# Interleaving the Strassen products of neighbouring feed-forward units in the pairs whose C11 came first

## The chip, the cores and the metric

The kernel runs on one core of a Trainium2 chip. The metric is the time of one execution on the device in microseconds (us). The version before the change takes 1913.47 us, the median of three runs (1908.57 to 1915.0). TensorE (PE in the profile) does the matrix products and writes them to PSUM, VectorE (DVE) and ScalarE (ACT) move and combine data, GpSimd (POOL) and SyncE (SP) issue transfers here.

## The reference

One decoder layer over 1024 tokens of width 1024, in float32: a SwiGLU feed-forward block added at half weight, a mixing block (dilated windowed attention beside a latent attention), and a second SwiGLU block.

```
h = rms(x, g)
x = x + 0.5 * (silu(h @ w_gate) * (h @ w_up)) @ w_down      # D_MODEL 1024, D_FF 2816
x = x + W_out [rms(dilated(h)) ; rms(mla(h))]
x = x + 0.5 * swiglu_2(rms(x))
```

The change touches only the gate and up products of the two feed-forward blocks, which the same function `ffn` computes twice.

## The kernel before

**Split products.** Each float32 product is made of three TensorE products in a faster number format: `split` (lines 99 to 102) makes a high part on ScalarE (L101) and the rest on VectorE (L102, called the low part below), and `products` (lines 117 to 127) multiplies high by high, high by low and low by high (L122, L124, L126). A 128x512 result with four blocks of depth is so 12 matmuls into one PSUM bank; `product` does this for one weight operand.

**Seven products instead of eight.** Gate and up weights are taken in 11 pairs (c = 0 to 10) of 128-column blocks; a pair has two units, gate "g" and up "u". For each unit the two column blocks, the two halves of the depth and the two halves of the tokens form a 2x2 by 2x2 block product, and Winograd's form of Strassen's scheme needs seven products for it: M11, M12, S1, S3, S2, S4, M22. The names are those of the weight operands. S1 to S4 are sums of weight blocks that VectorE makes (L328): S1 = M21 + M22, S3 = M11 - M21, S2 = S1 - M11, S4 = M12 - S2. The other factors (B11, B21, B22, T1 to T4) are kept for all 11 pairs.

**Two kinds of pairs.** For the first four pairs (c < FRONT = 4) the M11 and M12 products are done ahead, in `front`, since they need only the first half of the tokens; the product M11 is stored to DRAM (p1) for later. The middle stage then does five products for each unit of these pairs, 60 matmuls. Pairs 4 to 10 do all seven in the middle stage, 84 matmuls for a unit.

**A unit in the middle stage.** `middle` takes two PSUM banks, Dk and E, does S1 into Dk, S3 into E and S2 into a third bank A. Then VectorE reads: a = stored M11 (a tile `kept`, fetched by a POOL transfer, L579) + A (L586), q = a + E (L587), q = q + Dk (L588). `close` goes on in the same banks: S4 is added on top of Dk, and M22 on top of E, so these two products may begin only when L588 and L587 have read the banks. VectorE adds a to each (L596, L600). ScalarE applies the SiLU to the gate's four results (L604), and `finish` multiplies gate and up (L373), forms sums for the later down product (L385 to L388) and stores them with POOL transfers (L377, L383, L389, L390).

**Order.** `order` is a list of all weight operands in the order in which the products use them. `prepare` makes operands up to six products ahead of their use; making S1 of a unit also asks for the raw weights of the next unit (two transfers of 512 KB on SP's queue, L286). `behind_operands` puts the reads of PSUM on VectorE behind the low part of the operand three products on. The matmuls are issued in program order; the other engines' instructions are ordered by the compiler's scheduler. Buffers come from pools: 47 SBUF slots of 4 KB a partition, 12 smaller temporaries (`tmp`), 8 PSUM banks.

**The order in pairs 0 to 3 before.** For each unit in turn: S1, S3, S2, S4, M22. The last unit of a pair, u, is closed by `close_up` at the head of the next pair, directly behind its S2. Pairs 4 to 10 have 24 matmuls of another unit's M11 and M12 between S2 and S4 of a unit.

Of the kernel before, what the change touches and what calls it, by code (L numbers as in the profile page):

```python
# [18 lines left out]
P = 128  # L19
# [4 lines left out]
NF = DFF // P  # L24
# [25 lines left out]
FRONT = 4  # L50
# [11 lines left out]
def tile_layer(ctx: ExitStack, tc: tile.TileContext, x, g1n, mixn, g2n, wg1, wu1, wd1, wg2, wu2, wd2,  # L62
# [27 lines left out]
    def tmp(shape, dt=F32):  # L90
        return tpool.tile(shape, dt, tag="tmp", name=nm("tmp"))
# [131 lines left out]
    def ffn(rows_in, ys, gain, wg, wu, wd, act_d, xsrc, done, lead, aside=iter(())):  # L223
# [66 lines left out]
        PAIRS = range(NF // 2)  # L290
        order = [(c + i, m, w) for c in range(0, FRONT, 2) for w in ("M11", "M12") for i in range(2) for m in "gu"]
        for c in PAIRS:
            if c >= FRONT:
                order += [(c, "g", w) for w in ("M11", "M12")]
            if c > 0:
                order += [(c - 1, "u", w) for w in ("S4", "M22")]
            order += [(c, "g", w) for w in ("S1", "S3", "S2")]
            if c >= FRONT:
                order += [(c, "u", w) for w in ("M11", "M12")]
            order += [(c, "g", w) for w in ("S4", "M22")]  # L300
            order += [(c, "u", w) for w in ("S1", "S3", "S2")]
        order += [(NF // 2 - 1, "u", w) for w in ("S4", "M22")]
        units = [(True, c, m) for c in range(FRONT) for m in "gu"] + [(False, c, m) for c in PAIRS for m in "gu"]
        raws, sums_, ready = {}, {}, {}
# [8 lines left out]
        def make(c, nme, which):  # L313
            front = c < FRONT and which in ("M11", "M12")
            u = (front, c, nme)
            load_units(units.index(u) + (3 if front else 2))
            f1, f2 = raws[u][0], raws[u][-1]
            m = {"M11": f1[:, :512], "M12": f1[:, 512:], "M21": f2[:, :512], "M22": f2[:, 512:]}
            need = {"S1": ("M21", "M22", ALU.add), "S2": ("S1", "M11", ALU.subtract),
                    "S3": ("M11", "M21", ALU.subtract), "S4": ("M12", "S2", ALU.subtract)}  # L320
            if which in need:

                a_, b_, op = need[which]
                if which == "S1":
                    sums_["S1"] = tmp([P, 512])
                s1 = sums_["S1"]
                src = {"S1": s1, "S3": m["M21"], "S2": s1, "S4": m["M12"]}[which]
                nc.vector.tensor_tensor(src, s1 if a_ == "S1" else m[a_], s1 if b_ == "S2" else m[b_], op=op)  # L328
            else:
                src = m[which]  # L330
            s = slot([P, 2, 512], F32R)
            lows.append(split(s[:, 0, :], s[:, 1, :], src))
            ready[(c, nme, which)] = (s[:, 0, :], s[:, 1, :])
            if which == "M22" or (front and which == "M12"):
                del raws[u]
# [13 lines left out]
        def product(pt, c, nme, which, blk, first=True, ahead=AHEAD):  # L349
            assert order[used[0]] == (c, nme, which)  # L350
            prepare(ahead + 1)
            used[0] += 1
            w = ready.pop((c, nme, which))
            products(pt, [(cut(w, k * P, (k + 1) * P), blk.hi_lo(k)) for k in range(4)], first,
                     tc.keep_in_program_order)
# [3 lines left out]
        def finish(f, th, gate, up):  # L359

            c, j = f // 2, f % 2
            if c not in acts:
                acts[c] = {}
            two = acts[c]
            key = "diagonal" if j == th else "other"
            if c < FRONT and j == th == 0:
                early = tmp([P, 512])
                nc.vector.tensor_tensor(early, gate, up, op=ALU.mult)
                nc.gpsimd.dma_start(act_d[0, c], early)
                return  # L370
            if key not in two:
                two[key] = [slot([P, 2, 512]), 0]
            nc.vector.tensor_tensor(two[key][0][:, th if j == th else j, :], gate, up, op=ALU.mult)  # L373
            two[key][1] += 1
            if key == "diagonal" and c < FRONT:
                nc.gpsimd.dma_start(two[key][0][:, 0, :], act_d[0, c])
                nc.gpsimd.dma_start(act_d[3, c], two[key][0][:, 1, :])  # L377
                two[key][1] = 2
            elif key == "diagonal" and two[key][1] == 2:
                nc.gpsimd.dma_start(act_d[0:4:3, c].rearrange("s p t -> p s t"), two[key][0])  # L380
            if len(two) == 2 and two["diagonal"][1] + two["other"][1] == 4:
                (a11, a22), (a21, a12) = ([two[x][0][:, i, :] for i in range(2)] for x in ("diagonal", "other"))
                nc.gpsimd.dma_start(act_d[1, c], a12)  # L383
                s12, s43 = slot([P, 2, 512]), slot([P, 2, 512])
                nc.vector.tensor_tensor(s12[:, 0, :], a21, a22, op=ALU.add)  # L385
                nc.vector.tensor_tensor(s12[:, 1, :], s12[:, 0, :], a11, op=ALU.subtract)
                nc.vector.tensor_tensor(s43[:, 1, :], a11, a21, op=ALU.subtract)
                nc.vector.tensor_tensor(s43[:, 0, :], a12, s12[:, 1, :], op=ALU.subtract)  # L388
                nc.gpsimd.dma_start(act_d[4:6, c].rearrange("s p t -> p s t"), s12)  # L389
                nc.gpsimd.dma_start(act_d[2:7:4, c].rearrange("s p t -> p s t"), s43)  # L390
                del acts[c]
# [169 lines left out]
        def start(c, nme):  # L561

            A, Bk = ps(), ps()
            product(A, c, nme, "M11", B11)
            product(Bk, c, nme, "M12", B21)
            q = tmp([P, 512])
            nc.scalar.activation(q, A, AF.Copy)
            with behind_operands():
                nc.vector.tensor_tensor(q, q, Bk, op=ALU.add)  # L569
            return A, q  # L570

        def middle(c, nme, A):

            Dk, E = ps(), ps()
            product(Dk, c, nme, "S1", T1)
            product(E, c, nme, "S3", T3)
            if c < FRONT:
                A, kept = ps(), tmp([P, 512])
                nc.gpsimd.dma_start(kept, p1_d[c, :, "gu".index(nme), :])  # L579
            product(A, c, nme, "S2", T2, first=c < FRONT)  # L580
            a, q = tmp([P, 512]), tmp([P, 512])
            if c >= FRONT:
                nc.scalar.activation(a, A, AF.Copy)  # L583
            with behind_operands():
                if c < FRONT:
                    nc.vector.tensor_tensor(a, kept, A, op=ALU.add)  # L586
                nc.vector.tensor_tensor(q, a, E, op=ALU.add)  # L587
                nc.vector.tensor_tensor(q, q, Dk, op=ALU.add)  # L588
            return Dk, E, a, q

        def close(c, nme, Dk, E, a, between):

            product(Dk, c, nme, "S4", B22, first=False)
            q = tmp([P, 512])
            with behind_operands():
                nc.vector.tensor_tensor(q, a, Dk, op=ALU.add)  # L596
            between(q)
            product(E, c, nme, "M22", T4, first=False)
            with behind_operands():
                nc.vector.tensor_tensor(a, a, E, op=ALU.add)  # L600
            return q, a

        def silu(q):
            nc.scalar.activation(q, q, AF.Silu)  # L604

        def close_up(c, Dk, E, a, g12, g21):
            _, q = close(c, "u", Dk, E, a, lambda q: finish(2 * c, 1, g12, q))
            finish(2 * c + 1, 0, g21, q)

        late = None  # L610
        for c in PAIRS:
            if c in (4, 6):
                next(aside, None)
            A = Au = None
            if c >= FRONT:
                A, g11 = start(c, "g")
                silu(g11)
            if late:
                close_up(*late)
            Dk, E, a, g22 = middle(c, "g", A)  # L620
            silu(g22)
            if c >= FRONT:
                Au, u11 = start(c, "u")
                finish(2 * c, 0, g11, u11)
            if c == NF // 2 - 1:
                B11.t = B21.t = None
                for _ in range(2):
                    load_down(*loads.pop(0))
            g12, g21 = close(c, "g", Dk, E, a, silu)
            silu(g21)  # L630
            if c == KD - 1:
                fetch(2)
                for _ in range(PRELOAD - 2):
                    load_down(*loads.pop(0))
            Du, Eu, au, u22 = middle(c, "u", Au)
            finish(2 * c + 1, 1, g22, u22)
            late = (c, Du, Eu, au, g12, g21)
# [800 lines left out]
```

## Time and profile before

| what | before |
|---|---|
| median of three runs | 1913.47 us |
| the profiled execution, its own time | 1916.01 us |
| its span, first to last instruction | 1914.2 us |
| TensorE busy | 1835.1 us (96%) |
| VectorE busy | 1245.8 us (65%) |
| ScalarE busy | 793.8 us (41%) |
| mean granted TensorE clock | 0.983 |

The middle stage of pairs 0 to 3 is at about 62 to 206 us of the span in the first feed-forward block and at about 1287 to 1428 us in the second. In a timeline row the first number is the start and the second the duration in us, then engine, line, operation, tiles and count; the bracket says how long the engine had stood idle and whose end released it. In a row of windows stand the stretch, its length, the busy time of the engine with its instructions in brackets, and PEclk, the granted TensorE clock as a share of full speed. A row of waits ends with total us, count and the longest.

### The profile page before, as it was taken

Reading aid. Unit: us, or ns where it says so; the run is one execution under the profiler, and the core shown is the slowest. Engines: PE = TensorE matmul, PEld = TensorE weight load, DVE = VectorE, ACT = ScalarE, POOL = GpSimd, SP = SyncE. Lnnn points to the kernel's source line nnn. Section 1 sums busy time; section 2 is a strip of 40 time slices with the busy share of each in tenths; the row PEclk is TensorE's granted clock in tenths of the full one; section 3 lists DMA queues with packets and bytes.
Section 4 is the critical chain, followed back from the end, with each engine's and each line's share of the span. In section 5 each row is a group of like instructions: output and inputs, shape, how many; then the busy total and the mean of one; then the engine's idle time right before and its main releaser. Section 6 shows DMA issues by size and latency. Waiting matters only on the chain.

```text
span 1914.2 us, 25117 instructions
## 1 busy us (share of the span) xinstructions
PE 1835.1 (96%) x9040; PEld 1548.7 (81%) x9040; DVE 1245.8 (65%) x2375; ACT 793.8 (41%) x1802; POOL 294.8 (15%) x508
## 2 busy tenths in 40 slices
PE   8888999999999999999998999997889999999998
PEld 6666888888888888889998988886678888888887
DVE  6857666665978273327888783467657665778671
ACT  7412323333445153235875672453223333334540
POOL 3011010000000022323354520211000000000000
PEclk9889999999999999999999999998999999999999
DMA  7334224324954241023311332333432332288422
GB/s 253 116 105 156 92 90 138 131 84 176 356 172 127 94 137 33 28 55 117 89 36 30 93 118 77 125 130 117 131 109 96 119 105 94 84 305 310 126 56 88
DMA packets 92326, 234.38 MB, mean 122 GB/s; under 512 B 12487, under 2 KB 18329, under 8 KB 92201
## 3 DMA queue, kind: packets, MB, share of 16 engines
q1 hardware_dynamic: 71592, 162.93, 26.3%
q0 software_dynamic: 20608, 69.85, 10.4%
q8 instruction: 71, 1.16, 0.2%
q14 instruction: 55, 0.44, 0.1%
HBM read 165.00 MB, written 63.53 MB: 119 GB/s over the span
## 4 chain that ended last, share of the span: by engine, by line
PE 85%; DVE 9%; ACT 2%; issue 2%; DMA 2%; POOL 1%; SPq 0%; DVEq 0%; ACTq 0%; POOLq 0%
PE ps L122 18%; PE ps L124 18%; PE ps L126 18%; PE ps L520 7%; PE ps L519 7%; PE ps L518 7%; DVE slot L102 2%; PE ps L847 2%; PE ps L873 1%; PE ps L821 1%; PE ps L912 1%; ACT slot L101 1%; PE ps L837 1%; PE ps L1035 1%; DMA slot<-in_wu_dram 1%
## 5 line engine op out<-in xcount | busy, mean ns | idle before, releaser
L122 PE MATMUL ps<-slot,slot 128*128 128x512 f32 (+3 forms) x1712 | 668.4, 391 | 48.7 <-DVE tmp L588 31.8
L124 PE MATMUL ps<-slot,slot 128*128 128x512 f32 (+3 forms) x1712 | 662.1, 387 | 3.6 <-DVE slot L102 3.6
L126 PE MATMUL ps<-slot,slot 128*128 128x512 f32 (+3 forms) x1712 | 661.5, 387 | 0.0
L122 PEld LDWEIGHTS ps<-slot,slot 128*128 128x128 f32 x1712 | 327.1, 191 | 118.5 <-issue 36.5
L124 PEld LDWEIGHTS ps<-slot,slot 128*128 128x128 f32 x1712 | 327.8, 191 | 66.6 <-DVE slot L102 4.4
L126 PEld LDWEIGHTS ps<-slot,slot 128*128 128x128 f32 x1712 | 326.7, 191 | 63.9
L102 DVE TENSOR_TENSOR slot<-slot,slot 128x512 fp32r<-128x512 f32 (+1 forms) x428 | 294.4, 704 | 36.1 <-ACT slot L101 33.9
L101 ACT ACTIVATE slot<-slot 128x512 fp32r<-128x512 f32 (+1 forms) x428 | 260.7, 638 | 104.3 <-PE ps L520 44.8
L101 ACT ACTIVATE slot<-tmp 128x512 fp32r<-128x512 f32 x258 | 160.5, 626 | 314.1 <-DVE tmp L328 211.0
L519 PE MATMUL ps<-slot,slot 128*128 128x512 f32 x616 | 239.8, 390 | 0.0
L520 PE MATMUL ps<-slot,slot 128*128 128x512 f32 x616 | 239.5, 389 | 0.0
L518 PE MATMUL ps<-slot,slot 128*128 128x512 f32 x616 | 237.1, 389 | 0.0
L102 DVE TENSOR_TENSOR slot<-tmp,slot 128x512 fp32r<-128x512 f32 x258 | 176.4, 687 | 21.6 <-ACT slot L101 21.3
L520 PEld LDWEIGHTS ps<-slot,slot 128*128 128x128 f32 x616 | 115.7, 188 | 24.1
L519 PEld LDWEIGHTS ps<-slot,slot 128*128 128x128 f32 x616 | 115.7, 188 | 23.9
L518 PEld LDWEIGHTS ps<-slot,slot 128*128 128x128 f32 x616 | 115.7, 188 | 23.8
L604 ACT ACTIVATE tmp<-tmp 128x512 f32<-128x512 f32 x80 | 50.6, 632 | 185.9 <-DVE tmp L596 87.5
L526 DVE SCALAR_TENSOR_TENSOR slot<-ps,slot 128x512 f32<-128x512 f32 x56 | 37.4, 688 | 81.4 <-PE ps L520 81.2
L596 DVE TENSOR_TENSOR tmp<-tmp,ps 128x512 f32<-128x512 f32 x44 | 30.3, 688 | 80.3 <-PE ps L126 79.8
L587 DVE TENSOR_TENSOR tmp<-tmp,ps 128x512 f32<-128x512 f32 x44 | 30.2, 686 | 65.4 <-ACT tmp L583 65.2
L569 DVE TENSOR_TENSOR tmp<-tmp,ps 128x512 f32<-128x512 f32 x28 | 19.3, 688 | 81.4 <-PE ps L126 81.4
L829 ACT ACTIVATE slot<-slot,tmp 128x256 f32<-128x256 f32 (+1 forms) x128 | 59.7, 468 | 27.2 <-DVE tmp L822 26.4
(180 smaller groups left out, 2033.6 us busy)
## 6 DMA issues: line engine op xcount, KB each, us to landing
tmp<-act SPq DMA_DIRECT2D x154, 256.0 KB
act<-slot POOLq DMA_DIRECT2D x58, 512.0 KB, 5.2
slot<-in_wg_dram SPq DMA_DIRECT2D x52, 512.0 KB
slot<-in_wu_dram SPq DMA_DIRECT2D x52, 512.0 KB
slot<-in_wd_dram SPq DMA_DIRECT2D x40, 512.0 KB
slot<-in_x_dram SPq DMA_DIRECT2D x16, 512.0 KB
x_mid<-slot POOLq DMA_DIRECT2D x16, 512.0 KB, 4.1
slot<-x_mid SPq DMA_DIRECT2D x16, 512.0 KB
```

Source lines behind the costliest of these rows:

```text
L101: nc.scalar.activation(hi, src, AF.Copy)
L102: return nc.vector.tensor_tensor(lo, src, hi.bitcast(F32), op=ALU.subtract)
L122: pin(nc.tensor.matmul(pt, ah, bh, start=first and i == 0, stop=False, skip_group_check=not first))
L124: pin(nc.tensor.matmul(pt, ah, bl, start=False, stop=False, skip_group_check=not first))
L126: pin(nc.tensor.matmul(pt, al, bh, start=False, stop=i == total - 1, skip_group_check=not first))
L518: nc.tensor.matmul(banks[i], ah, w[:, 0, :], start=first and k == 0, stop=False, skip_group_check=not first)
L519: nc.tensor.matmul(banks[i], ah, w[:, 1, :], start=False, stop=False, skip_group_check=not first)
L520: nc.tensor.matmul(banks[i], al, w[:, 0, :], start=False, stop=k == KD - 1, skip_group_check=not first)
L526: nc.vector.scalar_tensor_tensor(xv, pt, 0.5, xv, op0=ALU.mult, op1=ALU.add)
L604: nc.scalar.activation(q, q, AF.Silu)
L829: nc.scalar.activation(self.p[:, e, :w], self.p[:, e, :w], AF.Exp, bias=self.m[e], scale=-1.0, accum_out=self.den[e])
L847: nc.tensor.matmul(po[:, e * HD:(e + 1) * HD], self.pt[:, n * P:(n + 1) * P], self.head["values"](self.far, self.j, e, j - nb + 1), start= ...
```

## The change

In pairs 0 to 3 the products are put in another order. Each unit does S1 and S3; then come S4 and M22 of the unit before it; then its own S2. `middle` gets a function `between` that is called between S3 and S2: in the gate's turn it closes the preceding pair's up unit (`close_up`), in the up's turn the same pair's gate unit (`close_gate`). The first unit has none before it, and the last, u of pair 3, is closed in pair 4 as before. The sum S1 is kept for each unit (`sums_[u]`), since two are now alive at once. The number of products, sums, reads and transfers is unchanged, and pairs 4 to 10 keep their order.

```
@@ order
+            if c < FRONT:
+                for m in "gu":
+                    order += [(c, m, w) for w in ("S1", "S3")]
+                    if (c, m) != (0, "g"):
+                        order += [(c, "g", w) if m == "u" else (c - 1, "u", w) for w in ("S4", "M22")]
+                    order.append((c, m, "S2"))
+                continue
+            order += [(c, "g", w) for w in ("M11", "M12")]
+            order += [(c - 1, "u", w) for w in ("S4", "M22")]
             order += [(c, "g", w) for w in ("S1", "S3", "S2")]
...
@@ make
                 if which == "S1":
-                    sums_["S1"] = tmp([P, 512])
-                s1 = sums_["S1"]
+                    sums_[u] = tmp([P, 512])
+                s1 = sums_[u]
...
-        def middle(c, nme, A):
+        def middle(c, nme, A, between=lambda: None):
             Dk, E = ps(), ps()
             product(Dk, c, nme, "S1", T1)
             product(E, c, nme, "S3", T3)
+            between()
             if c < FRONT:
                 A, kept = ps(), tmp([P, 512])
                 nc.gpsimd.dma_start(kept, p1_d[c, :, "gu".index(nme), :])
...
-        late = None
-        for c in PAIRS:
...
+        late, part = None, {}
+        def close_gate():
+            part["g12"], part["g21"] = close(*part.pop("g"), silu)
+            silu(part["g21"])
+        for c in range(FRONT):
...
+            Dk, E, a, g22 = middle(c, "g", None, lambda: late and close_up(*late))
+            silu(g22)
+            part["g"] = (c, "g", Dk, E, a)
+            Du, Eu, au, u22 = middle(c, "u", None, close_gate)
+            finish(2 * c + 1, 1, g22, u22)
+            late = (c, Du, Eu, au, part["g12"], part["g21"])
+        for c in range(FRONT, NF // 2):
...
+            A, g11 = start(c, "g")
+            silu(g11)
+            close_up(*late)
             Dk, E, a, g22 = middle(c, "g", A)
             silu(g22)
...
```

More of the change, by code (lines that the diff above doesn't have):

```diff
@@ L292, in ffn @@
         for c in PAIRS:
[L293 to L296, printed above, removed]
+            if c < FRONT:
[7 more added lines that the diff above has]
+            order += [(c - 1, "u", w) for w in ("S4", "M22")]
             order += [(c, "g", w) for w in ("S1", "S3", "S2")]
-            if c >= FRONT:
-                order += [(c, "u", w) for w in ("M11", "M12")]
+            order += [(c, "u", w) for w in ("M11", "M12")]
             order += [(c, "g", w) for w in ("S4", "M22")]
@@ L608, in close_up @@
             finish(2 * c + 1, 0, g21, q)
-        late = None
-        for c in PAIRS:
+        late, part = None, {}
[3 more added lines that the diff above has]
+        for c in range(FRONT):
             if c in (4, 6):
                 next(aside, None)
[L614 to L619, printed above, removed]
+            Dk, E, a, g22 = middle(c, "g", None, lambda: late and close_up(*late))
[5 more added lines that the diff above has]
+        for c in range(FRONT, NF // 2):
+            if c in (4, 6):
+                next(aside, None)
+            A, g11 = start(c, "g")
+            silu(g11)
+            close_up(*late)
             Dk, E, a, g22 = middle(c, "g", A)
             silu(g22)
-            if c >= FRONT:
-                Au, u11 = start(c, "u")
-                finish(2 * c, 0, g11, u11)
+            Au, u11 = start(c, "u")
+            finish(2 * c, 0, g11, u11)
             if c == NF // 2 - 1:
```

## The prediction

> **What bounds the kernel now.** I read the page's head first, then what TensorE waits for over the whole span, then the clock.
>
> ```profile
> span 1914.2 us, 25117 instructions
> PE 1835.1 (96%) x9040; PEld 1548.7 (81%) x9040; DVE 1245.8 (65%) x2375; ACT 793.8 (41%) x1802; POOL 294.8 (15%) x508
> PEclk9889999999999999999999999998999999999999
> ```
>
> ```profile
> PE ps L122 <- DVE tmp L588: 31.8, 12, 3.3
> PE ps L122 <- ACT slot L101: 13.7, 2, 7.5
> ```
>
> TensorE is busy 96% of the span, so it sets the end, and what can be won by another order is where it stands still or runs below its clock. Its largest wait for one line is for L588, the last VectorE read of the bank Dk: 31.8 us in 12 places. The clock row has its low digits in the second and third slice (48 to 144 us) and in one near 1390 us, that is, in both middle stages. One such place, TensorE and VectorE together:
>
> ```profile
> 151.52 0.39 PE L126 MATMUL ps<-slot,slot 128*128 128x512 f32 x1
> 151.95 0.69 DVE L586 TENSOR_TENSOR tmp<-tmp,ps 128x512 f32<-128x512 f32 x1 [0.34 <-PE ps L126]
> 152.55 0.69 DVE L102 TENSOR_TENSOR slot<-slot,slot 128x512 fp32r<-128x512 f32 x1
> 153.15 0.68 DVE L587 TENSOR_TENSOR tmp<-tmp,ps 128x512 f32<-128x512 f32 x1
> 153.87 0.69 DVE L588 TENSOR_TENSOR tmp<-tmp,ps 128x512 f32<-128x512 f32 x1
> 154.70 0.77 PE L122 MATMUL ps<-slot,slot 128*128 128x512 f32 x1 [2.79 <-DVE tmp L588]
> 157.76 0.40 PE L124 MATMUL ps<-slot,slot 128*128 128x512 f32 x1
> ```
>
> S2 ends at 151.91; L586, L587 and L588 follow one another on VectorE, and only then may S4 add to Dk, 2.79 us later. After that, matmuls start 0.43 us apart until 157.76, where they were 0.23 us apart before: the clock had gone down in the wait.
>
> To weigh both together I cut the stage into stretches of one unit, from the start of one S4 to that of the next, 60 matmuls each. The first row is an undisturbed stretch of 60 matmuls; two sums close the seven stretches of each block, 80.21 to 205.94 and 1306.95 to 1427.67.
>
> ```profile
> 200.01:213.61 13.60, 13.60 (x62) 1.00 0.11 40
> ...
> 80.21:99.12 18.91, 16.59 (x60) 0.85 0.18 56
> 99.12:117.36 18.24, 15.45 (x61) 0.89 0.56 182
> ...
> 189.51:205.94 16.43, 16.43 (x61) 0.83 0.22 68
> sum 125.73, PE 109.85; mean PE 15.69
> ...
> 1306.95:1325.22 18.27, 15.96 (x60) 0.87 0.19 58
> ...
> 1343.40:1359.55 16.15, 13.84 (x60) 1.00 0.22 72
> ...
> 1411.25:1427.67 16.42, 16.42 (x60) 0.82 0.20 74
> sum 120.72, PE 104.85; mean PE 14.98
> ```
>
> 14 stretches take 125.73 + 120.72 = 246.45 us, where 14 x 13.60 = 190.4 us would do: 56.05 us are lost. 31.8 of them are the 12 waits, the other 24.25 us are matmuls at a lower clock (a last stretch, 16.43 us, has no wait in it and loses 2.83 us by the clock alone).
>
> **The change, term by term.** Number of matmuls, VectorE operations and transfers: unchanged, cost 0.
>
> *Term 1, the 12 waits for L588: 31.8 us off.* Behind S2 now come S1 and S3 of the next unit, 24 matmuls or 24 x 13.60 / 60 = 5.44 us, in banks of their own. The longest wait so far was 3.3 us. The cover is 2.1 us longer than that, so S4 should find Dk read. If the cover failed, each place would cost its 2.3 to 3.3 us again. E is read by L587, earlier still.
>
> *Term 2, the low clock behind these waits.* The slow matmuls of the first stretch of each block belong to another wait (term 3). In it:
>
> ```profile
> 99.12 0.47 PE L122 MATMUL ps<-slot,slot 128*128 128x512 f32 x1 [2.32 <-DVE tmp L588]
> ```
>
> ```profile
> 1325.22 0.77 PE L122 MATMUL ps<-slot,slot 128*128 128x512 f32 x1 [2.31 <-DVE tmp L588]
> ```
>
> 18.91 - 13.60 - 2.32 = 2.99 us and 18.27 - 13.60 - 2.31 = 2.36 us, together 5.35 us. So 24.25 - 5.35 = 18.9 us stand behind the 12 waits, and go with them. Bounds: 0, if the low clock had another cause, and 18.9. I take 18.9, since slow matmuls begin at the end of waits only, and undisturbed stretches show 1.00.
>
> The Trainium skill, page "TensorE: Matmul & The Clock Gate", section "Why this matters for your kernels", says otherwise about short waits: TensorE falls to half clock when it idles for more than about 3 us. By that, only the two waits of over 3.3 us explain their slow stretches (2.83 and 2.82 us), and the rest, 13.2 us, would stay. The trace does not agree: 2.32 us idle before 99.12 is followed by a stretch at 0.89, though 2.31 us before the stretch at 1343.40 is followed by one at 1.00.
>
> *Term 3, the first unit.* Here VectorE is behind with operands, and S4 of g0 stands far longer:
>
> ```profile
> 72.30 0.39 PE L126 MATMUL ps<-slot,slot 128*128 128x512 f32 x1
> 80.21 0.76 PE L122 MATMUL ps<-slot,slot 128*128 128x512 f32 x1 [7.53 <-ACT slot L101]
> ```
>
> ```profile
> 75.77 0.69 DVE L102 TENSOR_TENSOR slot<-tmp,slot 128x512 fp32r<-128x512 f32 x1
> ...
> 79.38 0.69 DVE L588 TENSOR_TENSOR tmp<-tmp,ps 128x512 f32<-128x512 f32 x1
> ```
>
> ```profile
> 1300.20 0.63 PE L126 MATMUL ps<-slot,slot 128*128 128x512 f32 x1
> 1306.95 0.77 PE L122 MATMUL ps<-slot,slot 128*128 128x512 f32 x1 [6.12 <-ACT slot L101]
> ```
>
> ```profile
> 1302.52 0.69 DVE L102 TENSOR_TENSOR slot<-tmp,slot 128x512 fp32r<-128x512 f32 x1
> ```
>
> The release is put down to ScalarE, but L588 ends at 80.07, 0.14 us before: the same wait, later. In the new order TensorE goes on with S1 of u0. Its low part is the row at 75.77; with the low parts of S4 and M22 of g0 no longer ahead of it (2 x 0.60 us, the spacing of the rows above), it is there at 75.77 + 0.69 - 1.2 = 75.3 us. 24 matmuls at the same slow start end at 75.3 + 5.44 + 2.99 = 83.7 us, after L588; before, 24 matmuls were done at 80.21 + 5.44 + 2.99 = 88.6. Gain 4.9 us. In the second block: 1302.0 + 7.80 against 1306.95 + 7.80, gain 4.9 us. Bounds for both: 0 (VectorE keeps the old order of operands and S1 comes no sooner than S4 did) and 13.7 + 5.35 = 19 us (no wait at all). I take 9.8.
>
> *Term 4, new waits.* VectorE must now do a pair in less time. Two units before:
>
> ```profile
> 136.32:172.18 35.86, 30.74 (x120) 24.59 (x120) 22.24 (x36) 7.97 (x13) 4.18 (x7) 0.90 0.38 125
> ```
>
> ```profile
> DVE tmp L596 <- PE ps L126: 8.0, 2, 4.6
> ```
>
> The third busy time is VectorE's: 22.24 us for a pair that TensorE will do in 2 x 13.60 = 27.2 us, 82%, and in the 35.86 us it waited 8.0 for S4 alone. It fits, but it works in order, and a read that waits for S4 or M22 (L596, L600) holds the operands behind it. Bounds: 0 and all 12 old waits back. I put in two of the fourteen places at 2.3 us, 4.6 us.
>
> Sum: 31.8 + 18.9 + 9.8 - 4.6 = 55.9 us. The profiled execution took 1916.0 us, so 1860.1; the median of the runs lies 2.5 us under it, so **1858 us**.
>
> **Rivals.**
>
> *VectorE becomes the bound in these pairs.* If it keeps only the 8.0 us of waits for S4, a pair takes 22.24 + 8.0 = 30.2 us, 3.0 more than TensorE, for 7 pairs (3.5 in each block) 21 us: 1879. For it speaks the order of its queue; against it, that the 12 waits for L588 all lie in the stretches above, and pairs 4 to 10, with the same reads and 24 matmuls in between, have none.
>
> *The stored M11 comes late.* `kept` (L579) now stands behind `between` in the program, so behind the stores of `finish` on POOL's queue, which wait for VectorE.
>
> ```profile
> 145.26 0.68 DVE L600 TENSOR_TENSOR tmp<-tmp,ps 128x512 f32<-128x512 f32 x1
> ```
>
> ```profile
> 137.84 0.54 POOL L579 DMA_DIRECT2D tmp<-p  x1
> ...
> 149.86 0.71 POOL L390 DMA_DIRECT2D act<-slot  x1 [0.53 <-DVE slot L388]
> 150.56 0.57 POOL L579 DMA_DIRECT2D tmp<-p  x1
> ```
>
> ```profile
> tmp<-p POOLq DMA_DIRECT2D x16, 256.0 KB, 4.1
> ```
>
> From L600 to L579 behind the stores are 5.3 us, and 4.1 to land: 9.4 us after M22's read. L586 wants it 2.7 us after (S2's length), so 6.7 late; cover less chain is 5.44 - 3.3 = 2.1, a wait of 4.6 us, with 18.9 / 12 = 1.6 us of low clock, in the three gate units behind a `close_up` in each block: 6 x 6.2 = 37 us, 1895. Against it: the row at 137.84 was issued ahead of the stores at 149.86, though they stood before it in the program already; nothing it needs has changed.
>
> *The low clock stays.* If slow matmuls behind the ten shorter waits have another cause, 18.9 less those of the last two stretches, 2.83 and 2.82 us, that is 13.2 us, are not won: 1871. For it speaks the stretch at 1343.40, full clock after a wait; against it, that no slow stretch begins without one. The Trainium skill's rule above would have it so.
>
> *It does not do what it says:* VectorE's scheduler puts other work in front of L586 until the 5.44 us are used up; then nothing is won but the first unit, at most: 1904 to 1913, about no change.
>
> *Slower: raw weights starve.* M22 of a unit is now nine operands behind its S1, not five, so its two raw slots are held longer, and the transfers for a coming unit wait for slots.
>
> ```profile
> DMA packets 92326, 234.38 MB, mean 122 GB/s; under 512 B 12487, under 2 KB 18329, under 8 KB 92201
> ```
>
> ```profile
> 126.00 3.05 SPq L286 DMA_DIRECT2D slot<-in_wg_dram  x2
> ```
>
> ```profile
> 159.72 0.68 DVE L328 TENSOR_TENSOR tmp<-slot 128x512 f32<-128x512 f32 x1
> ```
>
> If slots allowed only two units, weights would be asked for when M22 of the last but one is split: 3.05 us to issue, 1 MB at the page's mean 122 GB/s 8.6 us, sum and split three operations of 0.7 us: 13.7 us, against M22 and S2, 5.4 us, as cover. 8.3 + 1.6 us of low clock in 14 units is 139 us, less the 60.5 of terms 1 to 3: 1992. It decides when a unit waits over 60.5 / 14 = 4.3 us. Against it: weights asked for at 126.00 are first summed at 159.72, 33.7 us on. Four operands more cost 4 x 2.72 = 10.9 us of such a lead; at the new pace two units are 27.2 us, and 16 remain.
>
> **How the numbers follow.** Forecast 0.67 (its own range 1846 to 1872, term 4 between 0 and 14 and term 3 up to 15); VectorE as the bound 0.12; late M11 0.08; clock stays 0.04; no change 0.05; slower 0.04. A measurement of this kernel can tell about 0.3% from no change, 5.7 us. Faster is the first four, 0.91; the same 0.05; slower 0.04. The range takes in the forecast, the VectorE case and the clock case and leaves out late M11, no change and slower, 0.17: 1846 to 1886.
>
> **What would show it.** Right: the wait of L122 for L588 gone or down to one or two places; stretches of 60 matmuls at 13.6 to 14 us and PEclk at 1.00 from about 90 to 206 us; VectorE 80% busy there; the first block's down stage some 28 us earlier, the end 56. Wrong in term 1: L122 still waits for L588, or for L102 or L101 instead. Wrong in term 2: no waits, but PEclk under 0.95. Late M11: L586 waits for a transfer, and L579 stands behind L390. Starving: L328 waits for a transfer from the weights.

## The result

The changed kernel takes 1850.99 us, the median of four executions (1850.05 to 1852.3), beside 1911.49 us for the kernel before on the same chip (1908.57 to 1915.0). The ratio is 0.9683, with a 95% interval of 0.9663 to 0.9704: 60.5 us faster, where 1858 us were forecast from 1913.47, 55.5 us. Two executions far outside the others, one of the kernel before at 2076.64 us and one of the kernel with useless matmuls (below) at 3766.56 us, are left out of all that follows.

The page of the changed kernel, its first lines and its clock row:

```profile
span 1848.6 us, 25118 instructions
PE 1812.8 (98%) x9040; PEld 1536.4 (83%) x9040; DVE 1241.5 (67%) x2375; ACT 791.5 (43%) x1802; POOL 295.1 (16%) x508
PEclk9999999999999999999999999999999999999999
```

The span is 65.6 us shorter, and the low digits of the clock row are gone. L588 of the kernel before is L593 now. The waits of TensorE over the whole span that belong to the middle stages are these (engine, line, whom it waited for, total us, count, longest):

```profile
PE ps L124 <- DVE slot L102: 4.8, 2, 2.4
PE ps L122 <- DVE tmp L593: 2.1, 2, 1.1
```

Of 12 waits for the last read of Dk, 31.8 us, and two longer ones in the first units, 13.7 us, two of 1.1 us are left. The two for T2's low part, in the first row, were 3.6 us before. Windows of the changed kernel, from the one wait for T2's low part in each block (in S2 of g0) to the start of pair 4, then one unit, then two units with VectorE's busy time in third place:

```profile
69.83:170.50 100.67, 99.60 (x431) 0.98 0.44 153
1261.15:1361.82 100.67, 99.60 (x430) 0.98 0.44 152
sum 201.34, PE 199.20; mean PE 99.60
...
94.35:107.95 13.60, 13.60 (x62) 1.00 0.62 212
...
81.00:108.20 27.20, 27.20 (x121) 22.48 (x121) 23.33 (x39) 9.36 (x17) 4.20 (x7) 1.00 0.33 112
```

The same stretches of the kernel before:

```profile
69.90:205.94 136.04, 112.63 (x432) 0.87 0.36 115
1296.64:1427.67 131.03, 109.04 (x431) 0.91 0.36 119
sum 267.07, PE 221.67; mean PE 110.83
```

267.07 - 201.34 = 65.7 us: the whole difference of the two spans lies in the two stretches that the change touches. From the first S4 on, a unit takes 13.60 us, which is what 60 matmuls take with nothing in the way. One place where the kernel before stood 2.3 to 3.3 us, now (VectorE's first and last read behind S2 of u0, and the first matmul of the S4 that needs them):

```profile
89.22 0.69 DVE L591 TENSOR_TENSOR tmp<-tmp,ps 128x512 f32<-128x512 f32 x1 [2.03 <-PE ps L126]
...
91.15 0.68 DVE L593 TENSOR_TENSOR tmp<-tmp,ps 128x512 f32<-128x512 f32 x1
```

```profile
94.47 0.39 PE L122 MATMUL ps<-slot,slot 128*128 128x512 f32 x1
```

The chain is as long as before, 2.6 us from the start of L591; it ends at 91.83, 2.6 us before S4, and TensorE does not stop for it. Only the head of the stage still has gaps:

```profile
69.83 0.50 PE L124 MATMUL ps<-slot,slot 128*128 128x512 f32 x1 [2.39 <-DVE slot L102]
...
74.05 0.39 PE L122 MATMUL ps<-slot,slot 128*128 128x512 f32 x1
...
80.75 0.47 PE L122 MATMUL ps<-slot,slot 128*128 128x512 f32 x1 [1.07 <-DVE tmp L593]
```

```profile
69.09 3.09 DVE L102 TENSOR_TENSOR slot<-tmp,slot 128x512 fp32r<-128x512 f32 x5
...
79.92 0.67 DVE L593 TENSOR_TENSOR tmp<-tmp,ps 128x512 f32<-128x512 f32 x1
```

The first row is inside S2 of g0; S1 of u0 begins at 74.05, straight behind it, since its low part is among the five that end at 72.18. The last row is the first S4.

### The profile page after: what moved, and what is told of

It is laid out like the page before. It is cut to its first block, busy times and chain, and to the rows that moved or that the text cites. A ratio compares the mean times of both kernels' runs of the same rounds, so it can differ in the third digit from the quotient of the medians.

```text
span 1848.6 us, 25118 instructions
## 1 busy us (share of the span) xinstructions
PE 1812.8 (98%) x9040; PEld 1536.4 (83%) x9040; DVE 1241.5 (67%) x2375; ACT 791.5 (43%) x1802; POOL 295.1 (16%) x508
## 4 chain that ended last, share of the span: by engine, by line
PE 89%; DVE 7%; ACT 2%; issue 1%; POOL 1%; DMA 0%; DVEq 0%; POOLq 0%; ACTq 0%
PE ps L122 19%; PE ps L124 19%; PE ps L126 19%; PE ps L523 7%; PE ps L524 7%; PE ps L522 7%; PE ps L864 2%; DVE slot L102 2%; PE ps L890 1%; PE ps L838 1%; PE ps L929 1%; PE ps L854 1%; PE ps L1052 1%; PE ps L234 1%; ACT slot L101 1%
## 5 line engine op out<-in xcount | busy, mean ns | idle before, releaser
L122 PE MATMUL ps<-slot,slot 128*128 128x512 f32 (+3 forms) x1712 | 659.2, 386 | 5.2 <-DVE tmp L593 2.1
L124 PE MATMUL ps<-slot,slot 128*128 128x512 f32 (+3 forms) x1712 | 655.4, 383 | 4.8 <-DVE slot L102 4.8
L126 PE MATMUL ps<-slot,slot 128*128 128x512 f32 (+3 forms) x1712 | 655.0, 383 | 0.0
L122 PEld LDWEIGHTS ps<-slot,slot 128*128 128x128 f32 x1712 | 322.4, 188 | 69.2 <-ACT slot L101 3.2
L124 PEld LDWEIGHTS ps<-slot,slot 128*128 128x128 f32 x1712 | 322.9, 189 | 66.7 <-DVE slot L102 5.6
L126 PEld LDWEIGHTS ps<-slot,slot 128*128 128x128 f32 x1712 | 322.7, 189 | 61.7
L101 ACT ACTIVATE slot<-slot 128x512 fp32r<-128x512 f32 (+1 forms) x428 | 260.0, 639 | 105.4 <-PE ps L524 49.0
L101 ACT ACTIVATE slot<-tmp 128x512 fp32r<-128x512 f32 x258 | 160.0, 625 | 282.8 <-DVE tmp L332 143.7
L524 PEld LDWEIGHTS ps<-slot,slot 128*128 128x128 f32 x616 | 115.7, 188 | 24.1
L522 PEld LDWEIGHTS ps<-slot,slot 128*128 128x128 f32 x616 | 115.6, 188 | 23.9
L523 PEld LDWEIGHTS ps<-slot,slot 128*128 128x128 f32 x616 | 115.7, 188 | 23.8
L592 DVE TENSOR_TENSOR tmp<-tmp,ps 128x512 f32<-128x512 f32 x44 | 30.2, 686 | 65.5 <-ACT tmp L588 65.2
L573 DVE TENSOR_TENSOR tmp<-tmp,ps 128x512 f32<-128x512 f32 x28 | 19.2, 687 | 81.5 <-PE ps L126 81.5
L136 POOL TENSOR_TENSOR small<-small,neghalf 128x1 f32<-128x1 f32 (+2 forms) x68 | 67.6, 997 | 5.0
```

Source lines behind the costliest of these rows:

```text
L101: nc.scalar.activation(hi, src, AF.Copy)
L122: pin(nc.tensor.matmul(pt, ah, bh, start=first and i == 0, stop=False, skip_group_check=not first))
L124: pin(nc.tensor.matmul(pt, ah, bl, start=False, stop=False, skip_group_check=not first))
L126: pin(nc.tensor.matmul(pt, al, bh, start=False, stop=i == total - 1, skip_group_check=not first))
L136: nc.gpsimd.tensor_tensor(r, r, neghalf[:, :w], op=ALU.pow)
L522: nc.tensor.matmul(banks[i], ah, w[:, 0, :], start=first and k == 0, stop=False, skip_group_check=not first)
```

## The experiments

Ratios stand to the kernel before, timed beside each. Its median was 1910.12 us beside the useless matmuls, pair 0 alone, the half cover and the first kernel on the head of the stage; 1912.36 beside the longer chains, the late M11 and T4 on POOL; 1913.78 and 1909.95 beside the last two pairs. The last read of Dk has another line number in each kernel; it is the `tmp<-tmp,ps` line that L122 waits for.

### Does the clock fall because TensorE stands still?

On the kernel before, with nothing of the change:

```
 def close(c, nme, Dk, E, a, between):
+    if c < FRONT and (c, nme) != (FRONT - 1, "u"):
+        spare, (hi, _) = ps(), B22.hi_lo(0)
+        for _ in range(10):
+            tc.keep_in_program_order(nc.tensor.matmul(spare, hi[:, :P], hi, start=True, stop=True))
```

> The old order, but ahead of each S4 that follows its own unit's S2 in pairs 0 to 3, ten matmuls (2.27 us at full clock) on operands long there go into a spare PSUM bank; nothing reads it. The waits for L588 stay as time (31.8 us), only TensorE no longer idles in them. Theory (the clock falls because TensorE idles): the 18.9 us of slow matmuls behind the 12 waits go, 1911.5 - 18.9 = 1893 us, granted clock of the stretches near 1.00; the first unit's long wait keeps its slow matmuls. Rival (the low clock has another cause): time stays at 1911 us or rises, clock 0.83 to 0.97 as before.

Measured: 1897.68 us, the median of three executions, ratio 0.9939 (0.9921 to 0.9957), 12.4 us faster with 140 matmuls more. In the trace the waits shrink to 4.3 us in six places, and a stretch of 141 matmuls over two old waits runs at full clock:

```profile
PE ps L122 <- DVE tmp L588: 4.3, 6, 1.1
```

```profile
115.78:148.61 32.83, 32.26 (x141) 1.00 0.40 135
```

So the low clock came from TensorE standing still, and filling the same time with useless matmuls removes it. The size is another matter: the span is 16.7 us shorter (1897.5 against 1914.2), near the 18.9 expected, but the medians differ by 12.4. The kernel before in its profiled execution, 1916.01 us, lay 4.5 us above its own median, so the 18.9 us read from it are more than usual.

### What is the first unit worth?

Pairs 1 to 3 in the old order:

```
+ if 0 < c < FRONT:
+     order += [(c - 1, "u", w) for w in ("S4", "M22")]
+     order += [(c, "g", w) for w in ("S1", "S3", "S2", "S4", "M22")]
+     order += [(c, "u", w) for w in ("S1", "S3", "S2")]
+     continue
...
+ if c > 0:
+     close_up(*late)
+     Dk, E, a, g22 = middle(c, "g", None)
...
+     close_gate()
+     Du, Eu, au, u22 = middle(c, "u", None)
```

> The new order in pair 0 alone; pairs 1 to 3 as before, so u0, g1, u1, g2, u2, g3 keep their S4 directly behind S2 and their six waits in each block. By the forecast the first unit gives 9.8 us: 1902 us. By a first reading of the changed trace it gives 15 us: 1896 us. Rival (most of the whole gain comes from the first unit): 1870 us or less.

Measured: 1897.29 us, ratio 0.9940 (0.9922 to 0.9959), 12.8 us. That lies between the two numbers and nearer to the second. TensorE's waits for the last read of Dk are back, the 12 old ones and two of 2.7 us at the first S4 of each block:

```profile
PE ps L122 <- DVE tmp L598: 37.1, 14, 3.3
```

About a fifth of the 60.5 us is the first units', the rest lies in the 12 places behind them.

### How much cover does it take?

S1 alone ahead of S4 and M22:

```
- order += [(c, m, w) for w in ("S1", "S3")]
+ order.append((c, m, "S1"))
  if (c, m) != (0, "g"):
      order += [... "S4", "M22"]
- order.append((c, m, "S2"))
+ order += [(c, m, w) for w in ("S3", "S2")]
...
  product(Dk, c, nme, "S1", T1)
+ between()
  product(E, c, nme, "S3", T3)
- between()
```

> The new order with only S1 of the next unit ahead of S4 and M22, S3 behind them: 12 matmuls, 2.72 us of cover instead of 5.44. Theory (the chain L586 to L588 is 2.3 to 3.3 us behind S2 and nothing else counts): waits of 0 to 0.6 us in each place, under 8 us in all, no slow matmuls, 1851 to 1859 us. Rival (VectorE puts operands between the reads, so that the longer cover is needed): waits of over 2 us with slow matmuls again, 1880 us or more.

Measured: 1867.38 us, ratio 0.9777 (0.9761 to 0.9792), 8 us over the upper end. Two kinds of places, the first S4 and a later one:

```profile
81.26 0.76 PE L122 MATMUL ps<-slot,slot 128*128 128x512 f32 x1 [3.96 <-ACT slot L101]
```

```profile
97.50 0.39 PE L126 MATMUL ps<-slot,slot 128*128 128x512 f32 x1
97.96 0.47 PE L122 MATMUL ps<-slot,slot 128*128 128x512 f32 x1
```

In five later places of each block S4 starts 0.46 us behind the matmul before it instead of 0.23: a chain of 2.9 us under a cover of 2.7, as the theory had it; the S4 of g3 waits 0.94 us. In the first unit the wait is 3.96 us instead of 1.07, and 13 matmuls behind it run 0.43 us apart. There VectorE has a backlog (shown below, with the head of the stage), and the second half of the cover is what it uses. The theory held for the steady places and left out the head.

The other way round, a longer chain under the full cover, made with ScalarE copies of `a` onto itself between the first and the second read:

```
  nc.vector.tensor_tensor(a, kept, A, op=ALU.add)
+ for _ in range(3):          # 7 in the second kernel
+     nc.scalar.activation(a, a, AF.Copy)
```

> The new kernel with three ScalarE copies of a onto itself between L591 and L592 in pairs 0 to 3: the chain behind S2 grows by about 3 x 0.65 = 2.0 us, VectorE gets no work. In the new trace L593 ends 2.4 us ahead of the S4 that needs it (91.83 against 94.35). Theory (5.44 us of cover, whatever the chain does within it): no new waits, 1851 us, at most 3 us more for the first unit. Rival (the order is tight and any later read shows): waits near 2 us in each place, 1880 us or more.

Measured: 1857.16 us, ratio 0.9710 (0.9679 to 0.9742), 5 to 6 us over the changed kernel instead of 0 to 3. Between the first S4 and that of g3 there is no gap in 359 matmuls:

```profile
81.95:163.81 81.86, 81.86 (x359) 1.00 0.40 140
```

```profile
PE ps L122 <- ACT slot L101: 4.0, 2, 2.0
PE ps L122 <- DVE tmp L595: 2.5, 2, 1.2
```

The chain is free as long as it stays in the cover. The two rows, 0.9 us more at each first S4 and 1.2 us at each S4 of g3, make 4.2 us; the rest, 1 to 2 us, is left open.

> The same with seven copies: the chain grows by 4.6 us, 2.2 us beyond the cover. Theory: L593 is waited for in all 14 places by about 2.2 us, 31 us, with 12 to 16 us of slow matmuls behind these waits: 1890 to 1900 us. If waits of this length do not bring the clock down: 1882 us.

Measured: 1917.74 us, ratio 1.0027 (1.0009 to 1.0044), 18 us over the upper end and slower than the kernel before.

```profile
102.62 0.68 DVE L595 TENSOR_TENSOR tmp<-tmp,ps 128x512 f32<-128x512 f32 x1
```

```profile
101.05 0.39 PE L126 MATMUL ps<-slot,slot 128*128 128x512 f32 x1
103.44 0.47 PE L122 MATMUL ps<-slot,slot 128*128 128x512 f32 x1 [2.00 <-ACT slot L101]
104.41 0.63 PE L122 MATMUL ps<-slot,slot 128*128 128x512 f32 x1
...
138.44 0.47 PE L122 MATMUL ps<-slot,slot 128*128 128x512 f32 x1 [2.00 <-ACT slot L101]
138.75 0.40 PE L124 MATMUL ps<-slot,slot 128*128 128x512 f32 x1
```

The steady waits are 2.0 us, as expected for 2.2. The release is put down to ScalarE (L101), but L595 ends 0.14 us before the S4 at 103.44: the chain of reads holds it. What was not reckoned is that the waits are not all alike: five reach 3.05 to 6.25 us, the longest ahead of the first S4 of each block, where the changed kernel already waits 1.07 us, and two more stand in pair 4, at the S4 of pair 3's last unit. Together they are 43.9 us in 16 places, where 31 in 14 were expected.

### Would a late fetch of the stored M11 have mattered?

```
+ stores.append(nc.gpsimd.dma_start(act_d[2:7:4, c].rearrange("s p t -> p s t"), s43))
...
+ if nme == "g" and c > 0:
+     with tc.issue_after(stores[-1].ins):
+         nc.gpsimd.dma_start(kept, p1_d[c, :, "gu".index(nme), :])
```

> The new kernel, but the fetch of the stored M11 of the gate units of pairs 1 to 3 (L584) is put on POOL's queue behind the last store of the preceding unit's finish, where the program has it. By the rival of the prediction: S4 of these three gates waits 4.6 us for the reads behind the fetch, with 1.6 us of slow matmuls, 6 x 6.2 = 37 us: 1888 us. If the cover is enough: 1851 us.

Measured: 1892.76 us, ratio 0.9893 (0.9867 to 0.9920), 42 us over the changed kernel where 37 were worked out. POOL's queue, then the first and last read, then TensorE:

```profile
104.15 0.72 POOL L394 DMA_DIRECT2D act<-slot  x1
105.01 0.57 POOL L586 DMA_DIRECT2D tmp<-p  x1
```

```profile
110.58 0.69 DVE L595 TENSOR_TENSOR tmp<-tmp,ps 128x512 f32<-128x512 f32 x1 [6.73 <-DMA tmp<-p]
...
112.51 0.68 DVE L597 TENSOR_TENSOR tmp<-tmp,ps 128x512 f32<-128x512 f32 x1
```

```profile
113.33 0.76 PE L122 MATMUL ps<-slot,slot 128*128 128x512 f32 x1 [5.00 <-ACT slot L101]
```

Here too the release is put down to ScalarE, but L597 ends 0.14 us before S4. The six waits are 4.47 to 8.28 us, where 4.6 each were worked out. The rival's mechanism is real and was priced about right; it just did not come. In the changed kernel the fetch for g1 is issued ahead of the stores, and L591 uses it at 102.93:

```profile
93.87 0.54 POOL L584 DMA_DIRECT2D tmp<-p  x1
102.70 0.74 POOL L393 DMA_DIRECT2D act<-slot  x1 [8.30 <-DVE slot L390]
```

### Can the head of the stage be made shorter?

Four attempts at the 2.4 us wait, its slow matmuls and the 1.07 us wait. In the first, pair 0 does S1 and S3 of both units, then both S2, then S4 and M22 of the gate:

```
+ if c == 0:
+     order += [(c, m, w) for m in "gu" for w in ("S1", "S3")]
+     order += [(c, m, "S2") for m in "gu"]
+     order += [(c, "g", w) for w in ("S4", "M22")]
+     continue
```

> The new order, except that pair 0 begins S1, S3 of the gate, S1, S3 of the up, then S2 of both, then S4 and M22 of the gate. Theory (the 2.4 us wait for T2's low part, its 1.7 us of slow matmuls and the 1.07 us wait ahead of the first S4 are an order of work, not a lack of VectorE time): all three go in both blocks, 2 x 5.2 = 10 us, 1841 us. Rival (VectorE, busy without a gap from 56 to 81 us, sets the head of the stage): the wait moves to another operand, 1850 us.

Measured: 1856.35 us, ratio 0.9724 (0.9707 to 0.9742), 5 us slower than the changed kernel. The waits are the old ones in other places:

```profile
PE ps L126 <- DVE slot L102: 5.5, 4, 2.4
PE ps L122 <- DVE tmp L603: 5.0, 2, 2.5
```

In the second, work is taken off VectorE:

```
- nc.vector.tensor_tensor(t, t, t1[k], op=ALU.subtract)
+ nc.gpsimd.tensor_tensor(t, t, t1[k], op=ALU.subtract)
  T4.put(k, t)
```

> The new kernel with the four subtractions that make T4 (L280) on POOL instead of VectorE: 4 x 0.60 = 2.4 us less on VectorE at the head of the stage, 4 x 1.3 us on POOL, which is idle there. Theory (VectorE, busy without a gap, sets the head): T2's low part comes 1.2 to 2.4 us sooner, the 2.4 us wait shrinks to 0 to 1.2 with its slow matmuls, and the 1.07 us wait goes: 1.2 to 5 us in each block, 1841 to 1849 us. Rival (the head waits for something else, or POOL's operations slow VectorE's down): 1851 us or more.

Measured: 1853.22 us, ratio 0.9691 (0.9663 to 0.9719), the rival. The reason is in two rows that overlap:

```profile
53.44 2.55 POOL L280 TENSOR_TENSOR slot<-slot,tmp 128x512 f32<-128x512 f32 x2
```

```profile
53.69 2.85 DVE L102 TENSOR_TENSOR slot<-slot,slot 128x512 fp32r<-128x512 f32 x1
56.47 0.68 DVE L102 TENSOR_TENSOR slot<-tmp,slot 128x512 fp32r<-128x512 f32 x1
```

While POOL does two subtractions, one VectorE operation of 0.69 us takes 2.85. Two operations of 0.60 us were saved there and 2.2 us lost; beside the other two subtractions an operation takes 1.77 us, and 1.1 are lost.

In the third, T2's parts come ahead of the sum S2 in the program; in the fourth, T4's eight VectorE operations also go behind S3 of u0:

```
  def hook_later(n):
+     if n == 5:
+         next(sums, None)      # T2
      prepare(5)
-     next(sums, None)
+     if n != 5:
+         next(sums, None)
...
  def close_gate():             # the fourth kernel only
+     if kept_t1:
+         make_t4()
+         kept_t1.clear()
```

> The new kernel with T2's high and low parts put ahead of the operand S2 of g0 in the program, so that ScalarE does not hold T2's high parts (idle until 65.06 for the sum S2). Theory (VectorE's total work sets the head of the stage): the 2.4 us wait for T2's low part goes, and the wait ahead of the first S4, now 1.07 us, grows by about as much as is won: 1848 to 1851 us. Rival (the head is a matter of order): both blocks win the wait and its 1.7 us of slow matmuls, 1843 us.

> The same, and T4's four subtractions and low parts (8 VectorE operations, 4.8 us, first needed by M22 of g0) put behind S3 of u0 in the program, so that L591 to L593 of g0 come up to 4.8 us sooner. Theory: no wait ahead of S2, S4 of g0 begins about 4 us sooner and only M22 may wait up to 2 us for T4: 2 to 5 us won in each block, 1841 to 1847 us. Rival (VectorE has no slack before M22 either): the wait moves to M22, 1849 us or more.

Measured: 1850.59 us, ratio 0.9670 (0.9655 to 0.9684), and 1848.53 us, ratio 0.9662 (0.9645 to 0.9679). In both kernels TensorE's largest wait in the middle stages is the same row:

```profile
PE ps L126 <- DVE slot L102: 6.0, 2, 3.0
```

The wait ahead of S4 is gone, but inside S2 of g0 TensorE now waits for the low part of the weight operand (L126), 3.0 us instead of 2.4 for T2's. To see whether the fourth is faster than the changed kernel at all, both ran once more side by side:

> The changed kernel itself, beside the next one on the same chip: 0.968 of the kernel before, as measured.

> T2 first and T4 late, now beside the changed kernel on one chip. If the 2 us between their medians on different calls are real: 1.5 to 3 us under the changed kernel. If they are the difference of chips: within 0.5 us of it.

Measured: 1849.52 and 1848.74 us, ratios 0.9677 (0.9653 to 0.9701) and 0.9670 (0.9645 to 0.9696). The 0.8 us between them lie between the two expectations and can't be told from none. No version that clearly beats the changed kernel was found.

The traces show what sets the head. These are the stretches from the stage's first matmul to the first S4, in the changed kernel, in its second run and in the kernel with S1 alone as cover; VectorE's busy time is the third:

```profile
61.61:80.75 19.14, 15.68 (x62) 12.17 (x60) 19.14 (x33) 8.20 (x16) 2.71 (x5) 0.91 0.49 170
...
62.19:81.32 19.13, 14.04 (x61) 11.03 (x60) 19.13 (x33) 8.20 (x16) 2.71 (x5) 1.00 0.50 172
...
62.13:81.26 19.13, 12.78 (x50) 9.83 (x48) 19.13 (x33) 8.73 (x17) 2.71 (x5) 0.89 0.50 178
```

VectorE has no gap in them, and S4 comes at 19.13 or 19.14 us whatever TensorE does meanwhile. In the second run of the changed kernel the 2.39 us wait for T2 brought no slow matmuls; the wait ahead of S4 was 2.70 us instead of 1.07, and nothing was won. So VectorE's work up to L593 sets the head, and the slow matmuls there cost nothing. In the fourth kernel, with eight operations moved from there, S4 has no wait ahead of it and comes at 17.27 to 19.83 us, by how many slow matmuls the 3.0 us wait brings; over the two blocks of its two traces the mean is 18.7, 0.4 us a block less, which fits the 0.8 us.

## Why the prediction was right

**Term 1, the 12 waits.** Right in mechanism and size: all 31.8 us are gone, and 2.6 us of the cover are unused, against 2.1 reckoned. The half cover and the longer chains show both sides: under 2.7 us of cover a place loses 0.2 us, a chain grown by three copies loses nothing in the steady places, one grown by seven loses 2.0.

**Term 2, the low clock.** The mechanism is shown by the useless matmuls. The size, 18.9 us, was that of one execution; in medians the same removal was worth 12.4 us, and about 2 us of that difference is the extra matmuls' own, since the span shrank by 16.7. The slow part varies from execution to execution. Each of the 35 executions of the kernel before that were timed beside the experiments has its granted clock on record: the 14 at 0.986 or more took 1906.9 to 1911.6 us, the 13 at 0.983 or less 1913.4 to 1919.7. The profiled one, at 0.983, was of the slower kind. One reading of the prediction is wrong: the wait before 1343.40 is 2.79 us, not 2.31. No slow matmuls follow it all the same; the last section shows why.

**Term 3, the first unit: mis-sized.** The stretches give 65.7 us in all; less 31.8 and 18.9, 15.0 us are left for it, a remainder, where 9.8 were put in. The step that failed is that the low part of S1 of u0 would be there at 75.3 us, two operations sooner than before. It was among the five low parts that end at 72.18, ahead of T4's, and S1 followed S2 at 74.05 without a gap. The new order let the scheduler put it before T4's parts too; the prediction had only moved it past the two operands that changed places with it. Measured alone, in medians, the first units are worth 12.8 us.

**Term 4, new waits: mis-sized.** 4.6 us were put in, and the steady units have none. VectorE is busy 23.33 of 27.20 us there, 86% where 82% was reckoned, and that leaves it enough time.

**The sum.** 55.9 us stood against 65.6 us in the spans and 60.5 in the medians. Terms 3 and 4 together were 9.8 us too small. What lay between the profiled execution and the median was taken as 2.5 us and was 4.5 before the change, 0.6 in the other direction after it; this took back half of the error. The mechanism was forecast; that the time came within 7 us of 1858 is in part luck, two terms too small beside a term read off a slow execution.

**The rivals.** VectorE did not become the bound in the steady units; at the head it is. It did not fill the cover with other work either, since L591 to L593 still take 2.6 us. The late M11, forced, costs 42 us, so that its price was fair and its chance the question. The page of the Trainium skill on the clock, "TensorE: Matmul & The Clock Gate", section "Why this matters for your kernels", was set against the rows: its limit of about 3 us would have left 13.2 us standing. They went with the waits, and the useless matmuls show that TensorE's idling was the cause. The raw weights were not late: in the changed kernel's stage VectorE, which reads them first, waits for TensorE alone, from 61 to 171 us 18.4 us in 11 places. That the weights starve was not tried by itself.

## What to carry to other kernels

A read of an accumulator that must be added to again is paid for twice on TensorE: once in the wait, and often again in slow matmuls behind it. Independent products put between the read and the next use remove both, and the chain of reads, measured from the profile, says how many are needed. Where the helper engine has a backlog, as at the head of a stage, the same cover is worth more than in the steady part, and the wait there moves rather than goes when the order is changed again. Before a term is read off one profiled execution, compare its time with the median: a part that varies between executions may be larger there than usual.

## What the runs showed of the hardware

Waits of 2.0 us can bring the clock down, and where they fall decides. In the kernel with seven copies, of two waits of 2.00 us, the one before 103.44 is followed by matmuls 0.43 us apart until 107.40, the one before 138.44 by none. In the changed kernel 2.39 us before 69.83 is followed by slow matmuls, 1.07 us before 80.75 by none; in its second run 2.39 us before 70.40 is followed by none.

In each of the 14 traces the stretches at half clock begin whole multiples of 3.41 us apart and, but for the one at the program's end, last 3.41, 6.83 or 10.24 us: the clock is granted in steps of 3.41 us. The steps that the two waits of 2.00 us fall into, each with the step behind it (length, TensorE's busy time, PEclk):

```profile
100.60:104.00 3.40, 1.40 (x7) 1.00 0.45 152
104.03:107.42 3.39, 3.39 (x10) 0.51 0.33 114
134.70:138.10 3.40, 1.74 (x8) 1.00 0.18 36
138.20:141.50 3.30, 3.06 (x14) 1.00 0.48 184
```

The first wait lies in one step, 2.00 us idle, and the next step is at half clock. The second is cut by the edge near 138.1 into 1.66 and 0.34 us. Over the 14 traces, from 10 us on and as long as matmuls were left to do, TensorE idled 1.99 us or more in 68 steps at full clock, and the next was at half clock behind all of them; with under 1.39 us idle it never was; between the two, behind 8 of 38. The edges lie elsewhere in each execution, so the same wait costs slow matmuls in one and none in another. The 2.79 us before 1343.40 were cut into 1.49 and 1.30 us.

POOL's subtraction of two 128x512 float32 operands in SBUF held back a VectorE operation of the same kind, 2.85 us instead of 0.69 while two of them ran. The Trainium skill, page "GPSIMD Engine Reference", section "Key points", says that the two engines share their SBUF interfaces and that VectorE operations with two SBUF inputs contend for them; the rows agree.
